# A feed-forward block's first chunk: two block products and the first out-projection matmuls are tied to a later place in TensorE's order

## The chip, the cores and the metric

The kernel runs on one core of one Trainium2 chip. The metric is the device time of one execution in microseconds (us), lower is better. Five things work side by side on the core: TensorE (PE in the profile, with PEld for its weight loads), VectorE (DVE), ScalarE (ACT), GpSimd (POOL) and SyncE (SP, which issues most loads). Each takes its own instructions in the order in which they stand, and waits at an instruction until what it needs is done.

## What is computed

One inference step of a two-layer encoder for 640 frames: 512 of a new stream and 8 times 16 of running streams. Layer 0 is a convolution module, layer 1 attends to shared keys and values, and each is followed by a SwiGLU feed-forward block. The change touches the feed-forward block alone:

```
def swiglu_ffn(h, g, w_in, w_out):
    a, b = jnp.split(rms_norm(h, g) @ w_in, 2, axis=-1)
    return h + (jax.nn.silu(a) * b) @ w_out
```

With D_MODEL = 1024 and FFN_HIDDEN = 2816, in float32. The block runs twice (once a layer).

## The kernel before

**Precision.** Every float32 product is three matmuls on parts that TensorE takes at full speed: a matrix is split into a high part (ACT copies it to a rounded type, line 374) and a low part (DVE subtracts, line 375), and hi*hi, lo*hi and hi*lo are summed in PSUM (line 442). The high and low parts of inputs are called XH and XL, of weights whi/wlo or shi/slo, of hidden tiles hid.

**Tiling.** `ffn` works on 22 hidden tiles of 128 features. Tiles 0 to 17 stand in three chunks of six, and each chunk is followed by its part of the out-projection. The two halves of the frames (320 columns each) and the two halves of the model dimension form a 2 by 2 block product, which is done with seven block products in place of eight (Strassen and Winograd's scheme, on combined inputs X11, X21, XT1 to XT4, X22). A block product is 4 k-steps of 3 matmuls: 12 matmuls of 128x320.

**Tiles 0 to 2** of the first chunk are done the plain way (`std`), since the combined inputs are not yet there. **Tiles 3, 4 and 5** are the first that use `seven`. One call of `seven` writes its block products in this order, with those of the tile ahead woven in: X11; XT4 of the tile ahead; X21; X22 of the tile ahead; XT2; XT1; XT3. The sums stand in two PSUM tiles: `pa` takes X11, then XT2 on top of it, then XT3, then XT4; `pe` takes XT1, then X22. Between them ACT copies `pa` out (`keep`, line 454): t1 after X11, t2 after XT2, t3 after XT3. Thus XT3 must not start before ACT has read t2, and XT4 not before it has read t3.

**Weights.** Each of these tiles brings 1 MB of weights (`raw`, one of two buffers, loaded by SP at line 417). DVE combines them in place (lines 425, 426, 428) with a sum `s` that POOL's two loads form (lines 420, 421), and ACT and DVE split the seven results into 11 small slots, used in turn. A raw buffer is loaded anew when its last reader is through. The third of these loads (tile 5) goes into the buffer of tile 3, then come the loads of the out-projection, of 768 KB each: group 0 into tile 4's buffer, group 1 into tile 5's, group 2 into group 0's, and so on.

**Order.** The code does not set each engine's order by itself. A scheduler orders each engine's instructions by priority and by a model of when each is ready; `tc.high_priority` lifts some, and `with behind(ins)` or `tc.issue_after(ins)` puts those of the block behind `ins` on the same engine, without a wait. The out-projection's own order is the table QORD, each step tied behind the one before by `last`; its first step in the table, `50'`, has none ahead.

Of the kernel before, what the change touches and what calls it, by code (L numbers as in the profile page):

```python
# [60 lines left out]
X11, X21, XT2, XT1, XT3, XT4, X22 = range(7)  # L61
# [24 lines left out]
def tile_trunk(ctx, tc, xT, vecs, hist, w_pw1, w_pw2, w_in0, w_out0, w_os0, w_in1, w_out1, w_os1,  # L86
# [21 lines left out]
    def mmt(n=512):  # L108
        return mm.tile([P, n], F32, tag="mm", name=nm("mm"))
# [29 lines left out]
    @contextmanager  # L139
    def behind(*ins):  # L140
        with ExitStack() as st:
            for i in ins:
                st.enter_context(tc.issue_after(i))
            yield
# [191 lines left out]
    def ffn(l, w_in, w_out, w_os, tail, hf, lead=(), b0=None, last_sum=()):  # L336
# [76 lines left out]
        def w_seven(src, out=False, first=(), rest=()):  # L413
            n = src.shape[-1] // 4
            raw, ws = wraw(), {}
            s1 = wx.tile([P, 512], F32, tag="s1", name=nm("s1"))[:, :n]
            nc.sync.dma_start(raw[:, :4 * n], src)
            a12, a11, a21, a22 = (raw[:, n * i:n * i + n] for i in range(4))
            with tc.high_priority(offset=HP), behind(*ties()):
                nc.gpsimd.dma_start(s1, src[:, 2 * n:3 * n])  # L420
                nc.gpsimd.dma_start(s1, src[:, 3 * n:4 * n], accum_op=add)
                for x in ((XT1, X11, X21, XT2, X22, XT3, XT4) if out else
                          (X11, X21, XT2, XT1, XT3, XT4, X22)):
                    if x == XT2:
                        nc.vector.tensor_tensor(out=a21, in0=a11, in1=a21, op=add)  # L425
                        nc.vector.tensor_tensor(out=a11, in0=s1, in1=a11, op=add)
                    elif x == X22:
                        nc.vector.tensor_tensor(out=a12, in0=a12, in1=a11, op=add)  # L428
                    ws[x] = slot()
                    with behind(*(first if x == XT1 else rest)):  # L430
                        cut(*ws[x], {XT1: s1, X11: a11, X21: a12, XT2: a11, X22: a12, XT3: a21,
                                     XT4: a22}[x])
            return ws

        def product(pt, w, xs, first, ks=None):
            (hi, lo), o0 = w
            n = len(xs)
            for k in ks or range(n):
                xh, xl = xs[k]
                c = slice(o0 + k * P, o0 + k * P + P)  # L440
                for i, (wt, v) in enumerate(((hi[:, c], xh), (lo[:, c], xh), (hi[:, c], xl))):
                    last = nc.tensor.matmul(pt, wt, v, start=(first and k == i == 0),  # L442
                                            stop=(k == n - 1 and i == 2), skip_group_check=True)
            return last

        def xproduct(pt, w, x, first):
            return product(pt, w, [(XH[x][:, k, :], XL[x][:, k, :]) for k in range(4)], first)
# [3 lines left out]
        def keep(tag, pt):  # L451
            t = tp.tile([P, NH], F32, tag=tag, name=nm(tag))
            with tc.high_priority(offset=HP):
                keeps.append(nc.scalar.activation(out=t, in_=pt, func=AF.Copy).ins)  # L454
            return t

        def plus(t, pt):
            with tc.high_priority(offset=HP):
                nc.vector.tensor_tensor(out=t, in0=pt, in1=t, op=add)  # L459

        def silu(t, src):
            with tc.high_priority(offset=HP):
                nc.scalar.activation(out=t, in_=src, func=AF.Silu)
# [27 lines left out]
        def combined(HH, HL, kp, second, held, neg, early=None):  # L491
# [32 lines left out]
                        own(XT4, b21)  # L524
            return sink

        def seven(src, sink, before):
            ws = w_seven(src)
            pa, pb = mmt()[:, :NH], mmt()[:, :NH]
            xproduct(pa, ws[X11], X11, True)  # L530
            t1 = keep("t1", pa)
            before(0)
            xproduct(pb, ws[X21], X21, True)
            plus(t1, pb)
            silu(t1, t1)
            before(1)
            xproduct(pa, ws[XT2], XT2, False)
            t2 = keep("t2", pa)
            pe = mmt()[:, :NH]
            xproduct(pe, ws[XT1], XT1, True)  # L540
            xproduct(pa, ws[XT3], XT3, False)
            t3 = keep("t3", pa)
            plus(t3, pe)

            def after(i):
                if i == 0:
                    last = xproduct(pa, ws[XT4], XT4, False)
                    sink(0, t1, pa)
                else:
                    last = xproduct(pe, ws[X22], X22, False)  # L550
                    plus(t2, pe)
                    silu(t2, t2)
                    sink(1, t2, t3)
                return last

            return after

        def out_chunk(c, HH, HL, after):
            ws, pts = {}, {}
            prod = {5: ("e", XT1, True, 1, 1), 1: ("a", X11, True, 0, 0),  # L560
                    2: ("b", X21, True, 0, 0), 6: ("a", XT2, False, 1, 0),
                    3: ("e", X22, False, 1, 0), 7: ("a", XT3, False, 1, 1),
                    4: ("a", XT4, False, 0, 1)}

            def go(i, u, part):
                if u not in ws:
                    o = (4 * c + u) * 12 * P
                    ws[u] = w_seven(w_os[:, o:o + 12 * P], True,
                                    (keeps[2:3], keeps[-2:-1])[u] if c == 0 and u < 2 else (),
                                    keeps[-1:] if (c, u) == (0, 1) else ())  # L570
                b, x, first, half, row = prod[i]
                if first and part != '"':
                    pts[b, u] = mmt()[:, :NH]
                pt = pts[b, u]
                with tc.issue_after(last[0]) if last else nullcontext():
                    ins = product(pt, ws[u][x], list(zip(HH[x], HL[x])), first,
                                  {"": None, "'": (0, 1), '"': (2,)}[part])
                last[:] = [ins.ins]
                if part == "'":
                    return  # L580
                hv = h[:, 2 * u + row, half * NH:half * NH + NH]
                with tc.high_priority(offset=HP):
                    nc.vector.tensor_tensor(out=hv, in0=hv, in1=pt, op=sub if row else add)  # L583

            last = []
            for t in QORD.split():
                if t[0] == "a":
                    with tc.issue_after(last[0]):
                        last[:] = [after(int(t[1])).ins]
                else:  # L590
                    go(int(t[0]), int(t[1]), t[2:])
            return lambda i: go((7, 4)[i], 3, "")
# [79 lines left out]
        for c in range(NCH):  # L672
            for jj in range(NSTD if c == 0 else 0, CW):
                if jj % 2 == 0:
                    held = [None] * 3
                if jj == NSTD and c == 0:
                    held = helds[1]
                after = seven(w_in[CW * c + jj], combined(HH, HL, jj // 2, jj % 2, held, True),
                              after)
            after = out_chunk(c, HH, HL, after)  # L680
            HH, HL = {}, {}
        hids = [(two(2 * jj), two(2 * jj + 1)) for jj in range(FT - NCH * CW)]
        for jj, hid in enumerate(hids):
            after = seven(w_in[NCH * CW + jj], plain(hid), after)
# [420 lines left out]
    for _ in ffn(0, w_in0, w_out0, w_os0, GR, hf, last_sum=last_sum)[1]:  # L1105
        pass
# [527 lines left out]
    for i in range(SPREAD_AT, KT):  # L1634
        with tc.issue_after(end):
# [4 lines left out]

    hf = ExitStack()
    spare, products = ffn(1, w_in1, w_out1, w_os1, ((256, 384), (0, 256)), hf,
                                     [(split_end[0], i) for i in (adds[1], adds[3], adds[5], sq_end)] +
                                     [(eps_end,)] * 2,
# [73 lines left out]
    last = [next(products) for _ in range(KT)][-1:]  # L1718
# [116 lines left out]
```

## Time and profile before

| | |
|---|---|
| median of 3 runs | 1445.59 us (1443.12 to 1446.67) |
| profiled execution | 1445.22 us, span 1443.4 us, granted TensorE clock 0.998 |
| PE busy | 1420.6 us (98%) |
| DVE busy | 1118.9 us (78%) |
| ACT busy | 748.6 us (52%) |
| first chunk, tiles 3 to 5 | from 285 us (first block), from 1051 us (second block) |

The first line of a page counts busy time. For a matmul that is a modelled time from start to end (0.31 us here), while the next one starts 0.147 us later, so a busy share near 100% says that PE is seldom idle for long and not that each matmul costs 0.31 us. Lost time on PE is therefore read from the distance of two starts. In a timeline a number in brackets is the engine's idle time ahead of that instruction, with what ended it; in a chain of waits each piece is what the end waited for at that time.

### The profile page before, as it was taken

How to read it: one execution, taken by the hardware profiler on the slowest of the kernel's cores; microseconds unless marked ns; L12 is line 12 of the kernel's file. 1: busy time of each engine (PE TensorE's matmuls, PEld its weight loads, DVE VectorE, ACT ScalarE, POOL GpSimd, SP SyncE). 2: the span in 40 equal slices, each digit the busy share in tenths (PEclk: the TensorE clock that was granted, in tenths of full speed). 3: DMA queues.
4: the chain of work that ended last, by engine and by line, in shares of the span. 5: the costliest groups of instructions: out<-in, count | busy, mean ns of one | idle time of the engine just before them, and what ended most of it. 6: DMA issues, size and time to landing. Idle time of an engine off the chain costs nothing. (4 is left out here: it accounts for less than half of the span.)

```text
span 1443.4 us, 28243 instructions
## 1 busy us (share of the span) xinstructions
PE 1420.6 (98%) x11086; PEld 1366.8 (95%) x11086; DVE 1118.9 (78%) x2490; ACT 748.6 (52%) x1633; POOL 284.3 (20%) x335
## 2 busy tenths in 40 slices
PE   9999999999999999999999999999999999999998
PEld 8998799999999999999998898988999999999998
DVE  6789867899788788766666756667899788888755
ACT  5666554564554554445654454543654564554443
POOL 5689221011111111013111111110011111111101
PEclk9999999999999999999999999999999999999999
DMA  7267524054435444524555555562034544444522
GB/s 246 70 174 190 137 76 135 24 141 134 138 103 143 133 110 122 146 91 162 174 183 195 191 176 166 183 220 67 30 98 134 157 111 123 132 116 124 148 60 74
DMA packets 66934, 192.58 MB, mean 133 GB/s; under 512 B 12145, under 2 KB 30321, under 8 KB 58481
## 3 DMA queue, kind: packets, MB, share of 16 engines
q1 hardware_dynamic: 52432, 160.58, 34.2%
q0 software_dynamic: 13504, 29.37, 10.3%
q8 instruction: 87, 1.43, 0.4%
q10 hardware_dynamic: 864, 0.83, 0.2%
q14 instruction: 47, 0.38, 0.1%
HBM read 179.14 MB, written 11.61 MB: 132 GB/s over the span
## 5 line engine op out<-in xcount | busy, mean ns | idle before, releaser
L442 PE MATMUL mm<-XH,whi 128*128 128x320 f32 x896 | 275.9, 310 | 2.6 <-ACT t L454 2.6
L442 PE MATMUL mm<-XH,wlo 128*128 128x320 f32 x896 | 276.3, 309 | 0.0
L442 PE MATMUL mm<-XL,whi 128*128 128x320 f32 x896 | 274.6, 309 | 0.0
L374 ACT ACTIVATE whi<-raw 128x512 fp32r<-128x512 f32 (+2 forms) x280 | 168.7, 613 | 139.4 <-PE mm L442 109.6
L375 DVE TENSOR_TENSOR wlo<-raw,whi 128x512 fp32r<-128x512 f32 (+2 forms) x280 | 184.6, 667 | 22.3 <-ACT whi L374 21.0
L442 PE MATMUL mm<-hid,whi 128*128 128x320 f32 x732 | 172.0, 310 | 3.7 <-DVE hid L375 2.7
L442 PEld LDWEIGHTS mm<-XH,whi 128*128 128x128 f32 x896 | 167.8, 188 | 4.2 <-ACT t L454 4.2
L442 PEld LDWEIGHTS mm<-XH,wlo 128*128 128x128 f32 x896 | 168.2, 188 | 0.0
L442 PEld LDWEIGHTS mm<-XL,whi 128*128 128x128 f32 x896 | 167.7, 188 | 0.0
L442 PEld LDWEIGHTS mm<-hid,whi 128*128 128x128 f32 x732 | 124.9, 188 | 6.4 <-DVE hid L375 3.7
L202 PE MATMUL mm<-xh,whi 128*128 128x320 f32 (+2 forms) x416 | 129.3, 313 | 1.0 <-ACT xh L190 0.6
L203 PE MATMUL mm<-xh,wlo 128*128 128x320 f32 (+2 forms) x416 | 128.0, 310 | 0.0
L204 PE MATMUL mm<-xl,whi 128*128 128x320 f32 (+2 forms) x416 | 126.0, 310 | 0.0
L442 PE MATMUL mm<-hid,wlo 128*128 128x320 f32 x366 | 113.0, 309 | 0.0
L442 PE MATMUL mm<-XH,shi 128*128 128x320 f32 x344 | 106.0, 309 | 0.7 <-DVE h L1548 0.7
L442 PE MATMUL mm<-XH,slo 128*128 128x320 f32 x344 | 106.0, 308 | 0.0
L442 PE MATMUL mm<-XL,shi 128*128 128x320 f32 x344 | 105.5, 308 | 0.0
L420 POOL DMA_DIRECT2D s<-in_w_in x38 | 22.1, 582 | 375.8 <-DVE wlo L375 152.8
L844 POOL TENSOR_TENSOR ca<-ca,cvt 128x512 f32<-128x512 f32 x60 | 91.8, 1531 | 17.4 <-ACT cvt L841 10.9
L374 ACT ACTIVATE shi<-raw 128x512 fp32r<-128x512 f32 (+1 forms) x114 | 66.7, 588 | 45.1 <-PE mm L442 39.6
L454 ACT ACTIVATE t<-mm 128x320 f32<-128x320 f32 x114 | 49.5, 434 | 66.8 <-PE mm L442 66.5
L583 DVE TENSOR_TENSOR h<-h,mm 128x320 f32<-128x320 f32 x168 | 79.9, 481 | 5.3 <-PE mm L442 5.1
(337 smaller groups left out, 3696.7 us busy)
## 6 DMA issues: line engine op xcount, KB each, us to landing
raw<-in_w_in SPq DMA_DIRECT2D x38, 1024.0 KB
s<-in_w_in POOLq DMA_DIRECT2D x76, 256.0 KB, 4.2
raw<-in_w_os SPq DMA_DIRECT2D x24, 768.0 KB
cache<-in_ck SPq DMA_DIRECT2D x32, 512.0 KB
cache<-in_cv SPq DMA_DIRECT2D x32, 512.0 KB
raw<-in_w_pw SPq DMA_DIRECT2D x11, 1024.0 KB
s<-in_w_os POOLq DMA_DIRECT2D x48, 192.0 KB, 3.6
raw<-in_w_kq SPq DMA_DIRECT2D x8, 1024.0 KB
```

The source lines that it names most:

```text
L202: nc.tensor.matmul(ps, wh, xh, start=(first and i == 0), stop=False)
L203: nc.tensor.matmul(ps, wl, xh, start=False, stop=False)
L204: end = nc.tensor.matmul(ps, wh, xl, start=False, stop=(stop and i == last))
L374: put_end[1] = nc.scalar.activation(out=hi, in_=src, func=AF.Copy).ins
L375: put_end[0] = nc.vector.tensor_tensor(out=lo, in0=src, in1=hi.bitcast(F32), op=sub).ins
L420: nc.gpsimd.dma_start(s1, src[:, 2 * n:3 * n])
L442: last = nc.tensor.matmul(pt, wt, v, start=(first and k == i == 0), stop=(k == n - 1 and i == 2), skip_group_check=True)
L454: keeps.append(nc.scalar.activation(out=t, in_=pt, func=AF.Copy).ins)
L583: nc.vector.tensor_tensor(out=hv, in0=hv, in1=pt, op=sub if row else add)
L844: nc.gpsimd.tensor_tensor(out=acc, in0=acc, in1=pr, op=ALU.add)
```

## The change

Three ties are added, and each has effect in the first chunk of both blocks. No instruction is added or removed.

```
--- before.py
+++ after.py
@@ -524,6 +524,12 @@
+        xt2_end, xt3_end = [], [None]
+
+        def tie(own):
+            xt2_end.append(own)
+            return {2: xt2_end[:1], 3: xt2_end[2:]}.get(len(xt2_end), ())
+
         def seven(src, sink, before):
...
@@ -534,11 +540,12 @@
             before(1)
-            xproduct(pa, ws[XT2], XT2, False)
+            own = xproduct(pa, ws[XT2], XT2, False).ins
             t2 = keep("t2", pa)
             pe = mmt()[:, :NH]
-            xproduct(pe, ws[XT1], XT1, True)
-            xproduct(pa, ws[XT3], XT3, False)
+            with behind(*tie(own)):
+                xproduct(pe, ws[XT1], XT1, True)
+            xt3_end[0] = xproduct(pa, ws[XT3], XT3, False).ins
             t3 = keep("t3", pa)
             plus(t3, pe)
@@ -582,7 +589,7 @@
-            last = []
+            last = [xt3_end[0]]
             for t in QORD.split():
```

Tile 4's XT1 now stands behind tile 3's XT2; tile 5's XT1 behind its own XT2; the out-projection's first step behind XT3 of the chunk's last tile. In later chunks the order comes out as before.

On PE, at XT3 of tile 3 in the second block: `mm_12638` is `pa` of tile 3, `mm_12819` is `pe` of tile 4, XH_1414 is XT2, XH_1416 is XT3, XH_1412 is XT1. Before:

```order
L442 MATMUL mm_12638<-XH_1414_12038,shi_12073 128x320
L442 MATMUL mm_12638<-XH_1414_12038,slo_12074 128x320
L442 MATMUL mm_12638<-XL_1415_12039,shi_12073 128x320
L442 MATMUL mm_12638<-XH_1416_12040,whi_12065 128x320 [waits Activation_49]
L442 MATMUL mm_12638<-XH_1416_12040,wlo_12066 128x320
```

The same place now:

```order
L442 MATMUL mm_12819<-XH_1412_12036,whi_12067 128x320
L442 MATMUL mm_12819<-XH_1412_12036,wlo_12068 128x320
L442 MATMUL mm_12819<-XL_1413_12037,whi_12067 128x320
L442 MATMUL mm_12638<-XH_1416_12040,whi_12065 128x320 [waits Activation_49]
L442 MATMUL mm_12638<-XH_1416_12040,wlo_12066 128x320
```

XT2 of tile 3 moved ahead of the 12 matmuls of tile 4's XT1, which now stand between XT2 and XT3 of tile 3. In the same way, 6 out-projection matmuls now stand between XT3 and XT4 of tile 5, where XT4 followed XT3 at once. Further, 8 matmuls of tile 5's X11 and X21 moved ahead of tile 4's XT3.

DVE's order follows, since the scheduler plans with PE's. On DVE in the second block, `raw_12847` is the raw buffer of tile 5, `raw_12980` that of the out-projection's group 0. The stretch up to the last reader of `raw_12847`, before:

```order
L428 TENSOR_TENSOR raw_12847<-raw_12847 128x512 [waits DVE_49]
L375 TENSOR_TENSOR slo_12070<-raw_12980,shi_12069 128x384 [waits Activation_49]
L375 TENSOR_TENSOR wlo_12066<-raw_12847,whi_12065 128x512 [waits Activation_49]
L459 TENSOR_TENSOR t_1514_12844<-mm_12819,t_1514_12844 128x320 [waits Activation_49]
L482 SCALAR_TENSOR_TENSOR B_1511_12792<-t_1502_12680,t_1504_12707 128x320 [waits Activation_49]
L426 TENSOR_TENSOR raw_12980<-s_1530_12981,raw_12980 128x384 [waits DVE_49]
L459 TENSOR_TENSOR t_1519_12883<-mm_12870,t_1519_12883 128x320 [waits PE_49,Activation_49]
L375 TENSOR_TENSOR wlo_12068<-raw_12847,whi_12067 128x512 [waits Activation_49]
```

and now:

```order
L428 TENSOR_TENSOR raw_12847<-raw_12847 128x512 [waits DVE_49]
L459 TENSOR_TENSOR t_1502_12680<-mm_12682,t_1502_12680 128x320 [waits PE_49]
L375 TENSOR_TENSOR wlo_12066<-raw_12847,whi_12065 128x512 [waits Activation_49]
L375 TENSOR_TENSOR wlo_12066<-s_1516_12848,whi_12065 128x512 [waits Activation_49]
L375 TENSOR_TENSOR hid_12244<-B_1510_12760,hid_12243 128x320 [waits Activation_49]
L375 TENSOR_TENSOR wlo_12068<-raw_12847,whi_12067 128x512 [waits Activation_49]
```

The last reader now stands ahead of five others (slo, t_1514, B_1511, raw_12980, t_1519). Its buffer takes group 1's weights (`raw_13100`) next.

Further on, DVE takes up group 2's weights (`raw_13203`), with the first two additions into h behind. Before:

```order
L428 TENSOR_TENSOR raw_13100<-raw_13100 128x384 [waits DVE_49]
L375 TENSOR_TENSOR wlo_12068<-raw_13100,whi_12067 128x384 [waits Activation_49]
L425 TENSOR_TENSOR raw_13203<-raw_13203 128x384 [waits DMAHW3_49]
L583 TENSOR_TENSOR h<-h,mm_13002 128x320 [waits PE_49]
L583 TENSOR_TENSOR h<-h,mm_13062 128x320 [waits PE_49]
```

and now (line 583 is 590 in the changed file):

```order
L428 TENSOR_TENSOR raw_13100<-raw_13100 128x384 [waits DVE_49]
L425 TENSOR_TENSOR raw_13203<-raw_13203 128x384 [waits DMAHW3_49]
L375 TENSOR_TENSOR wlo_12068<-raw_13100,whi_12067 128x384 [waits Activation_49]
L590 TENSOR_TENSOR h<-h,mm_13002 128x320 [waits PE_49]
L590 TENSOR_TENSOR h<-h,mm_13062 128x320 [waits PE_49]
```

The low part `wlo_12068` moved behind the instruction that waits for the load, ahead of the two additions. The take-up of group 1 (`raw_13100`, line 425) moved ahead too, by six places. SP's and POOL's orders are the same as before. The first block shows the same pieces with other numbers.

## The prediction

> **What bounds the kernel now.** The page first: PE is nearly always occupied, so only its gaps and what ends them can give time.
>
> ```profile
> PE 1420.6 (98%) x11086; PEld 1366.8 (95%) x11086; DVE 1118.9 (78%) x2490; ACT 748.6 (52%) x1633; POOL 284.3 (20%) x335
> ```
>
> Then PE's waits in the second block's first chunk (1058 to 1101 us): what, total us, times, longest. They add up to 2.7 us, and only the first row is for the copies that the change speaks of; the others wait for DVE's results.
>
> ```profile
> PE mm L442 <- ACT t L454: 1.1, 2, 0.5
> PE mm L442 <- DVE h L583: 0.8, 1, 0.8
> PE mm L442 <- DVE hid L375: 0.5, 1, 0.5
> PE mm L442 <- ACT hid L374: 0.3, 1, 0.3
> ```
>
> PE's timeline shows the first kind: XT2's last matmul and XT3's first two (first block), and XT4's first (second block).
>
> ```profile
> 297.15 0.31 PE L442 MATMUL mm<-XL,shi 128*128 128x320 f32 x1
> 297.98 0.41 PE L442 MATMUL mm<-XH,whi 128*128 128x320 f32 x1 [0.53 <-ACT t L454]
> 298.23 0.31 PE L442 MATMUL mm<-XH,wlo 128*128 128x320 f32 x1
> 298.38 0.31 PE L442 MATMUL mm<-XL,whi 128*128 128x320 f32 x1
> ...
> 1086.88 0.42 PE L442 MATMUL mm<-XH,whi 128*128 128x320 f32 x1 [0.53 <-ACT t L454]
> ```
>
> Undisturbed, starts are 0.147 us apart (298.23 to 298.38 reads 0.15). Here the distances are 0.83 and 0.25: a gap costs 0.69 + 0.10 = 0.79 us. There are four (XT3 of tile 3 and XT4 of tile 5, in two blocks): 3.2 us if PE alone decided.
>
> It doesn't. The chain of waits, second block:
>
> ```profile
> 1061.24 7.85 DMA raw<-in_w_in
> ...
> 1077.22 0.40 DVE B L482
> 1077.62 0.47 DVE raw L426
> 1078.09 0.40 DVE t L459
> 1078.49 0.61 DVE wlo L375
> ...
> 1079.12 5.47 DMA raw<-in_w_os
> ...
> 1087.41 5.70 DMA raw<-in_w_os
> ...
> 1098.75 103.56 PE mm L442 x703
> ```
>
> From 1061 to 1098.75 the end hangs on DVE and on loads that DVE's last readers release, PE in it only afterwards. The rows give DVE's pace too: 0.40 us for 320 columns, 0.47 for 384, 0.60 for 512.
>
> **The change, part by part.** It adds and removes no instruction; all cost is in waits.
>
> *XT2 of tile 3 goes ahead of 12 matmuls.* XT2 ends 12 x 0.147 = 1.76 us earlier, with two effects. First, ACT's copy of t2 is done before XT3 is due, behind the 12 matmuls: 0.79 us of PE gap goes in each block. The cover lasts 1.76 us, and the copy takes 0.44 (row 297.49). Second, ACT stands at that copy, with a weight split queued behind it for which DVE waits:
>
> ```profile
> 297.49 0.44 ACT L454 ACTIVATE t<-mm 128x320 f32<-128x320 f32 x1 [4.85 <-PE mm L442]
> 297.82 0.62 ACT L374 ACTIVATE shi<-raw 128x512 fp32r<-128x512 f32 x1
> ```
>
> In DVE's timeline of the second block that is the idle time at 1064.58; it goes 1.76 us earlier:
>
> ```profile
> 1064.58 0.69 DVE L375 TENSOR_TENSOR slo<-raw,shi 128x512 fp32r<-128x512 f32 x1 [2.17 <-ACT shi L374]
> ...
> 1069.11 0.69 DVE L425 TENSOR_TENSOR raw<-raw 128x512 f32<-128x512 f32 x1 [0.97 <-DMA raw<-in_w_in]
> 1069.78 0.69 DVE L375 TENSOR_TENSOR wlo<-raw,whi 128x512 fp32r<-128x512 f32 x1
> ...
> 1086.83 0.55 DVE L375 TENSOR_TENSOR wlo<-raw,whi 128x384 fp32r<-128x384 f32 x1
> ...
> 1093.13 0.56 DVE L425 TENSOR_TENSOR raw<-raw 128x384 f32<-128x384 f32 x1 [0.61 <-DMA raw<-in_w_os]
> 1093.61 0.88 DVE L583 TENSOR_TENSOR h<-h,mm 128x320 f32<-128x320 f32 x2
> ```
>
> But at 1069.11 DVE waits for tile 5's load, issued at 1061.24, when nothing has moved yet. So in the second block the 1.76 us only lengthen that wait. Gain on DVE there: nothing.
>
> *Second block from 1069.78.* DVE is dense to the end of this stretch, so its order alone counts. Up to the last reader of tile 5's raw buffer stand now 13 instructions, 9 x 0.60 + 3 x 0.40 + 0.47 = 7.07 us: it ends at 1076.9 (before, 1078.49 + 0.61 = 1079.1). Group 1's load is issued 2.2 us earlier and lands at 1076.9 + 5.5 = 1082.4 to 1082.5. But its take-up (line 425) also stands six places earlier: 12 instructions on, 8 x 0.40 + 4 x 0.47 = 5.08 us, at 1082.0. DVE waits some 0.5 us there, with all its work queued behind. Then come ten instructions and the take-up itself (4.8 us) up to the last reader of group 0's buffer: it ends at 1087.4, where it ended before (1086.83 + 0.55). That must be so: the same work from 1069.78, less one instruction of 0.40, plus the wait. Group 2's load is thus issued as before, and lands as before at 1093.1. Ahead of the additions into h now stands one `wlo` more (0.47), which before was done while DVE idled for 0.61. The additions come 0.45 us later, and PE, which waits for h and hid there, goes on 0.45 us later. With loads of 5.9 us (below, 312.31 to 318.21) it would be 1.0 later; with loads that land before DVE comes, 1.1 us earlier (the 0.40, the 0.61 and some 0.1 more). I take 0.45, since both loads have their own rows in this block.
>
> *6 matmuls between XT3 and XT4 of tile 5* cover 0.88 us, more than the 0.79. In the second block ACT's copy of t3 may be late:
>
> ```profile
> 1084.43 0.53 ACT L374 ACTIVATE whi<-s 128x384 fp32r<-128x384 f32 x1 [0.48 <-DMA s<-in_w_os]
> ...
> 1086.38 0.44 ACT L454 ACTIVATE t<-mm 128x320 f32<-128x320 f32 x1 [0.65 <-PE mm L442]
> ```
>
> Ahead of it ACT waits for POOL's load of s, and two more instructions follow, each behind DVE; so XT4 starts near 1086.5, not at 1085.4. PE's gain up to here (0.4 instead of 1.6 us) is anyway lost at the additions. The same holds of the 8 matmuls of tile 5 that go ahead of tile 4's XT3: they bring its copy and XT4 close (some 0.5 us of new wait in the second block), at no price while DVE decides.
>
> *First block.* Same chain, other state: DVE's rows, and SP's two issues.
>
> ```profile
> 301.96 0.69 DVE L425 TENSOR_TENSOR raw<-raw 128x512 f32<-128x512 f32 x1
> 302.79 0.69 DVE L375 TENSOR_TENSOR wlo<-raw,whi 128x512 fp32r<-128x512 f32 x1
> ...
> 318.21 0.56 DVE L425 TENSOR_TENSOR raw<-raw 128x384 f32<-128x384 f32 x1 [0.46 <-DMA raw<-in_w_os]
> ...
> 320.43 0.55 DVE L375 TENSOR_TENSOR wlo<-raw,whi 128x384 fp32r<-128x384 f32 x1
> ...
> 322.83 0.49 DVE L482 SCALAR_TENSOR_TENSOR B<-t,mm 128x320 f32<-128x320 f32 x1 [0.58 <-PE mm L442]
> ...
> 326.31 0.55 DVE L425 TENSOR_TENSOR raw<-raw 128x384 f32<-128x384 f32 x1
> 326.78 0.88 DVE L583 TENSOR_TENSOR h<-h,mm 128x320 f32<-128x320 f32 x2
> ```
>
> ```profile
> 312.31 0.33 SPq L417 DMA_DIRECT2D raw<-in_w_os  x1
> ...
> 321.02 0.33 SPq L417 DMA_DIRECT2D raw<-in_w_os  x1
> ```
>
> At 301.96 DVE didn't wait, so the load had landed; when, no row tells. DVE will come at 300.2. The gain is between 0 (landed just then) and 1.76. In the second block the same load needed all of 7.85 us, so I take it near the late end: 302.4 in place of 302.79 for the next row, 0.4 us. From there the work is 320.98 - 302.79 = 18.2 us, less the wait of 0.46, small ones of 0.1 and one instruction (0.40): 17.25. With a new wait of 0.45 at group 1's load (309.5 + 5.5 against DVE at 314.55), group 0's buffer is free at 320.1, 0.9 us earlier. Group 2's load needs at most 326.31 - 321.02 = 5.3 us. DVE comes at 324.8 (the wait of 0.58 for PE goes, since XT4 ends earlier), finds the load at 324.8 to 325.4, and begins the additions at 325.95 with the extra `wlo`, against 326.78: 0.8 us earlier. The ends: 1.6 (PE's two gaps, no more) and 0.1.
>
> *Sum.* -0.8 + 0.45 = -0.4 us, between -2.7 (-1.6 - 1.1) and +0.9 (-0.1 + 1.0). In later chunks PE runs without such waits (103.56 us in the last row of the chain), so what it has at the first chunk's end it keeps. Against the profiled execution's own 1445.2 us: 1444.8. The median of the runs is 0.4 higher, within their scatter of 1443.1 to 1446.7, which is added to the range.
>
> **The rivals.**
>
> *PE decides.* If the loads are there whenever DVE comes, all four gaps go and DVE's results come in time: -3.2, 1442.0. For it: the gaps are plain in the rows and PE's order is fixed when the kernel is built. Against: 0.97 us of waiting at 1069.11.
>
> *The out-projection's loads land sooner.* Issued 2.2 us earlier, group 1's load runs with less beside it. From 5.0 us down, neither load holds DVE up long: -1.6 and -1.1, together -2.7, 1442.5. Against: 5.47, 5.70 and 5.90 us in rows with different neighbours. The Trainium skill (DMA: Bandwidth & Descriptors, section on the anatomy of one DMA) gives, measured for loads of POOL's kind, about 2.0 us plus the bytes at 436 GB/s; taken for SP's loads that is an estimate of 3.8 us for 768 KB. By that rule this rival would hold in both blocks; the trace's rows are 1.7 us and more above it, so it gets little.
>
> *Slower: the early neighbour.* With the split at 1064.58 goes the last reader of tile 4's buffer, so group 0's load is also issued 1.76 us earlier, into tile 5's load, on which DVE waits. If the two share evenly for 1.76 us more, tile 5's weights land up to 0.88 later in each block: second block +1.3, first +0.1, together +1.4, 1446.6. It decides as soon as DVE's take-up comes later than 1069.5. The Trainium skill's same page (section on queues and rings) says that each DMA engine consumes one queue's descriptors in ring order. Both loads come from SP, so by that rule the early neighbour takes nothing; no row here settles it.
>
> **How the numbers follow.** Forecast 0.5; PE decides 0.15; sooner loads 0.12; early neighbour 0.18; something else 0.05. 1444.8 is the forecast's. The range reaches from the two gains to the neighbour, each with half the runs' scatter cut off: 1441.8 to 1447.2; the forecast's own is 1442.5 to 1446.1. A change of 0.3% (4.3 us) is about what a measurement of this kernel can tell. No case reaches it; the first two come within 1.6 us of it, with scatter: faster 0.06, slower 0.04, within 0.9.
>
> **What would show it.** Right: in both blocks no gap ahead of tile 3's XT3; DVE's split at 1064.58 about 1.8 us earlier, and its wait for tile 5's load in the second block near 2.7 us; a DVE wait of some 0.5 at group 1's take-up, and of 1 us at group 2's; PE's waits for h and hid in the second block longer by 1 to 2 us. Wrong: tile 5's load taken up clearly before or after 1069.1 (on the old time scale), or loads of 768 KB under 5 us, or PE waiting at places not named.

## The result and the profile after

| | before | changed |
|---|---|---|
| median of the timed runs | 1445.48 us | 1443.11 us |
| profiled execution's span | 1443.4 us | 1441.9 us |
| ratio | | 0.9985, 95% interval 0.998 to 0.9991 |

By the ratio the change gains 2.2 us, between 1.3 and 2.9 us (the two medians differ by 2.4). The forecast was a gain of 0.4, the lower bound of its sum a gain of 2.7: the sign was right, the size was not.

The page's first line and one of its groups, of the changed kernel. The last two columns of a group are the idle time of the engine just before these instructions, and what ended most of it:

```profile
PE 1420.6 (99%) x11086; PEld 1368.0 (95%) x11086; DVE 1119.8 (78%) x2490; ACT 749.3 (52%) x1633; POOL 283.5 (20%) x335
...
L442 PE MATMUL mm<-XH,whi 128*128 128x320 f32 x896 | 275.0, 310 | 0.5 <-ACT t L454 0.5
```

The same group before:

```profile
L442 PE MATMUL mm<-XH,whi 128*128 128x320 f32 x896 | 275.9, 310 | 2.6 <-ACT t L454 2.6
```

PE's waits for ACT's copies fell from 2.6 to 0.5 us: the four gaps are gone. In PE's waits in the second block's first chunk (1057 to 1105 us) no copy stands any longer, but h stands twice:

```profile
PE mm L442 <- DVE h L590: 1.2, 2, 0.8
PE mm L442 <- DVE hid L375: 0.5, 1, 0.5
PE mm L442 <- ACT hid L374: 0.3, 1, 0.3
```

The second of these two doesn't stand in the profile before. It is here in PE's timeline, behind the first additions:

```profile
1102.40 0.42 PE L442 MATMUL mm<-hid,whi 128*128 128x320 f32 x1 [0.80 <-DVE h L590]
```

Its start stands 1.12 us behind the one before it, where 0.15 is usual. DVE's timeline of the same stretch shows the rows that the prediction spoke of, and what is late at 1102.40:

```profile
1062.24 0.69 DVE L375 TENSOR_TENSOR slo<-raw,shi 128x512 fp32r<-128x512 f32 x1 [0.40 <-ACT shi L374]
...
1066.80 0.56 DVE L375 TENSOR_TENSOR wlo<-s,whi 128x384 fp32r<-128x384 f32 x1 [1.06 <-ACT whi L374]
1067.68 0.69 DVE L425 TENSOR_TENSOR raw<-raw 128x512 f32<-128x512 f32 x1 [0.32 <-DMA raw<-in_w_in]
...
1074.83 0.68 DVE L375 TENSOR_TENSOR wlo<-raw,whi 128x512 fp32r<-128x512 f32 x1
...
1080.52 0.55 DVE L425 TENSOR_TENSOR raw<-raw 128x384 f32<-128x384 f32 x1
...
1090.08 0.56 DVE L425 TENSOR_TENSOR raw<-raw 128x384 f32<-128x384 f32 x1
1090.56 0.55 DVE L375 TENSOR_TENSOR wlo<-raw,whi 128x384 fp32r<-128x384 f32 x1
1091.02 0.88 DVE L590 TENSOR_TENSOR h<-h,mm 128x320 f32<-128x320 f32 x2
...
1099.66 0.56 DVE L425 TENSOR_TENSOR raw<-raw 128x384 f32<-128x384 f32 x1 [2.34 <-DMA raw<-in_w_os]
```

SP issued the loads behind these take-ups (tile 5, then groups 1, 2 and 3) at:

```profile
1060.66 0.33 SPq L417 DMA_DIRECT2D raw<-in_w_in  x1
...
1075.54 0.33 SPq L417 DMA_DIRECT2D raw<-in_w_os  x1
...
1085.44 0.33 SPq L417 DMA_DIRECT2D raw<-in_w_os  x1
...
1093.73 0.33 SPq L417 DMA_DIRECT2D raw<-in_w_os  x1
```

The last reader at 1074.83 releases group 1's load at 1075.54. DVE takes it up 4.98 us later at 1080.52 and waits for nothing. The forecast had it land after 5.5 us, with a wait of 0.5 us. Group 2's load is there when DVE comes, 4.64 us after its issue (1090.08), where before it needed 5.70. So DVE doesn't wait from 1067.68 to the additions at 1091.02. That takes 23.34 us; before it took 24.50 (1069.11 to 1093.61). The next load takes 5.93 us, and DVE stands at its take-up for 2.34 us with additions queued behind.

The first block, the same rows of DVE:

```profile
301.67 0.69 DVE L425 TENSOR_TENSOR raw<-raw 128x512 f32<-128x512 f32 x1 [1.57 <-DMA raw<-in_w_in]
...
314.51 0.55 DVE L425 TENSOR_TENSOR raw<-raw 128x384 f32<-128x384 f32 x1
...
324.47 0.56 DVE L425 TENSOR_TENSOR raw<-raw 128x384 f32<-128x384 f32 x1 [0.38 <-DMA raw<-in_w_os]
325.41 0.88 DVE L590 TENSOR_TENSOR h<-h,mm 128x320 f32<-128x320 f32 x2
```

Here the same way takes 23.74 us, before 24.82 (301.96 to 326.78): 1.1 us less again.

**Where the time went.** PE does the same number of matmuls in nearly the same order in both kernels. So the start of each can be set against that of the same number in the trace before; the difference, followed through the trace, shows at which place PE wins or loses. It stands at -0.6 us where the first block's chunk begins (scatter between two executions). Then come -0.8 and -0.8 at the two gaps, +0.8 at the additions and +0.3 at group 3's take-up: -0.48 over the chunk. In the second block: -0.8 and -0.8, -0.4 at the additions, +1.1 at the new stall: -0.93. Between the blocks 1.0 us is lost at one place, where only the clock differs (last section). Below, "PE's balance" of a chunk is this difference from its start to its end.

### The profile page after: what moved, and what is told of

Read it like the earlier page. It is cut to its first block, busy times and chain, and to the rows that moved or that the text cites. A ratio compares the mean times of both kernels' runs of the same rounds, so it can differ in the third digit from the quotient of the medians.

```text
span 1441.9 us, 28247 instructions
## 1 busy us (share of the span) xinstructions
PE 1420.6 (99%) x11086; PEld 1368.0 (95%) x11086; DVE 1119.8 (78%) x2490; ACT 749.3 (52%) x1633; POOL 283.5 (20%) x335
## 4 chain that ended last, share of the span: by engine, by line
PE 84%; DVE 9%; DMA 4%; ACT 1%; issue 1%; POOL 1%; DVEq 0%; POOLq 0%; ACTq 0%
PE mm L442 42%; PE mm L1279 10%; PE mm L202 6%; PE mm L204 6%; PE mm L203 6%; PE mm L895 3%; DMA raw<-in_w_os 2%; PE w L1279 2%; DVE wlo L375 2%; DMA raw<-in_w_in 2%; PE am L1452 1%; PE am L1524 1%; PE am L1468 1%; PE w L1423 1%; DVE slo L375 1%
```

## Experiments

Theory A: DVE and the loads that it waits for set the end of the chunk. The gain is group 1's load, which is issued earlier and so runs clear of POOL's loads. Theory B: PE's own gaps are the gain. PE's balance, worked out from each trace against that of the kernel before, in us:

| kernel | block 1 | block 2 | timed ratio, 95% interval |
|---|---|---|---|
| the whole change | -0.48 | -0.93 | 0.9985 (0.998 to 0.9991) |
| out-projection's tie only | +0.13 | +0.82 | 0.9993 (0.9984 to 1.0002) |
| both block products only | -0.24 | -1.80 | 0.997 (0.9959 to 0.9982) |
| whole change, first block only | -1.00 | (+0.09) | 0.9986 (0.9977 to 0.9995) |
| whole change, second block only | (+0.22) | -1.44 | 0.9982 (0.9973 to 0.9991) |
| late last reader | +1.09 | -0.31 | 0.999 (0.9981 to 1.0) |
| group 3 taken up later | -1.30 | -2.08 | 0.9972 (0.9961 to 0.9983) |
| groups 2 and 3 later | -1.54 | -2.29 | 0.9971 (0.996 to 0.9981) |
| products only, group 2 later | -1.46 | -1.28 | 0.9965 (0.9953 to 0.9978) |
| light s loads | (+0.43) | (+0.15) | one run, 1444.86 us |
| group 3 later, no tie | -0.56 | -0.70 | 0.9994 (0.9985 to 1.0003) |
| tile 4's tie only | -1.36 | -1.51 | 0.9985 (0.9977 to 0.9994) |

In brackets are blocks with the order of before: they differ by up to 0.4 us by chance, and no single balance means more than that. Added up over both blocks, a kernel's balances miss its timed gain by up to 2.3 us (both block products only: -2.0 against -4.4). Averaged over the blocks that have the order of before (three each) and over those that have the order of the change (two each), the change wins 0.96 us in the first block and 1.26 in the second: 2.2 in all, the size of the timed gain.

**The out-projection's tie only.**

```
-            return {2: xt2_end[:1], 3: xt2_end[2:]}.get(len(xt2_end), ())
+            return ()
```

> Only the out-projection's first step is tied behind XT3 of tile 5; both block products stay where they were. On PE six matmuls move between XT3 and XT4 of tile 5, in both blocks, and no other engine's order changes. Theory A (DVE and the loads it waits for set the end of the first chunk, and the gain of the whole change comes from their order): the two gaps of 0.79 us ahead of XT4 go, PE waits as much longer for h right behind them, and the time stays: 0 us, within 0.3. Theory B (PE's own gaps are the gain): -1.6 us.

It gave 0.9993, -1.0 us (-2.3 to 0.3), which excludes neither. The edit was a poorer test than I thought. Its six matmuls stood ahead of XT3 of tile 5 before, and covered the copy of t2 there. In PE's timeline of the second block a new gap stands at XT3, and the wait for h at the additions swallows what is left:

```profile
1082.33 0.42 PE L442 MATMUL mm<-XH,whi 128*128 128x320 f32 x1 [0.29 <-ACT t L454]
...
1093.69 0.42 PE L442 MATMUL mm<-hid,shi 128*128 128x320 f32 x1 [1.84 <-DVE h L590]
```

DVE's order is that of before, and there is no gain in either block. That speaks for A, but group 2's load also happened to be late in this profile, which accounts for most of the 1.84:

```profile
1092.28 0.56 DVE L425 TENSOR_TENSOR raw<-raw 128x384 f32<-128x384 f32 x1 [1.67 <-DMA raw<-in_w_os]
```

**Both block products only.**

```
-            last = [xt3_end[0]]
+            last = []
```

> Only the two block products are tied (XT1 of tiles 4 and 5); the out-projection's first step is free as before. Up to the take-up of group 1's weights DVE's order is that of the whole change; PE keeps part of the gap ahead of XT4 of tile 5 (two matmuls of cover, 0.3 of 0.79 us). Theory A: about the whole change, -1.5 to -2.2 us, and group 1's load lands within 5.0 us of its issue. Theory B: the two gaps ahead of XT3 of tile 3 and 0.3 us of each other one: -2.2 us less what is given back. The trace decides: by A what PE has at its first wait for h is what DVE brings; by B it is the sum of its gaps.

It gave 0.997, a gain of 4.4 us (2.6 to 5.9), twice that of the whole change and more than either theory had forecast. Group 1's load was taken up 4.97 us after its issue in both blocks, as A had it. DVE's order is the same up to group 1's take-up; the scheduler put group 3's take-up three places later, behind two more additions. The experiments with the take-ups follow that up.

**One block at a time.**

```
-            return {2: xt2_end[:1], 3: xt2_end[2:]}.get(len(xt2_end), ())
+            return {2: xt2_end[:1], 3: xt2_end[2:]}.get(len(xt2_end), ()) if l == 0 else ()
...
-            last = [xt3_end[0]]
+            last = [xt3_end[0]] if l == 0 else []
```

and the same with `l == 1`.

> The whole change in the first block alone, the second as before. The prediction's sum: -0.8 us. From the two traces, aligned matmul by matmul: -0.9 us at the first block's end, nothing more behind. If the first block's gain were lost on the way to the second (the profile of the changed kernel gives back 1.0 us between 1000 and 1005 us): 0.

> The whole change in the second block alone, the first as before. The prediction's sum: +0.45 us. If loads that land sooner are what it missed: -0.9 us (PE 1.6 earlier at XT4 of tile 5, 2.0 at the first additions, 1.0 given back at the next group's load), with group 1's load of 768 KB taken up within 5.0 us of its issue.

Both gain: -2.0 us (-3.3 to -0.7) and -2.6 us (-3.9 to -1.3). The forecast of +0.45 for the second block alone is excluded. The two add up to more than the whole change did (-4.6 against -2.2); their traces add up to -2.4. What of this is scatter stays open. In the first block of the first kernel, which has the changed order, the 0.8 us that the changed kernel's profile loses at the additions is not lost: PE's start there is 0.24 us late, as before, in place of 1.04.

The first of these kernels has the old order in its second block. Its DVE rows there, for the take-ups of tile 5 and of groups 1, 2 and 3:

```profile
1067.31 0.69 DVE L425 TENSOR_TENSOR raw<-raw 128x512 f32<-128x512 f32 x1
...
1082.86 0.55 DVE L425 TENSOR_TENSOR raw<-raw 128x384 f32<-128x384 f32 x1
...
1091.52 0.55 DVE L425 TENSOR_TENSOR raw<-raw 128x384 f32<-128x384 f32 x1
...
1100.33 0.56 DVE L425 TENSOR_TENSOR raw<-raw 128x384 f32<-128x384 f32 x1 [2.05 <-DMA raw<-in_w_os]
```

In the profile before, the first and the third of these showed waits of 0.97 and 0.61 us. Here neither has one, and the fourth waits 2.05 in place of 0.84. The fourth in the profile before, second block and first:

```profile
1100.74 0.56 DVE L425 TENSOR_TENSOR raw<-raw 128x384 f32<-128x384 f32 x1 [0.84 <-DMA raw<-in_w_os]
...
334.89 0.56 DVE L425 TENSOR_TENSOR raw<-raw 128x384 f32<-128x384 f32 x1 [1.81 <-DMA raw<-in_w_os]
```

The instructions are the same, and so is the end of the chunk within 0.1 us. Waits for loads of this kind pass from one take-up to another between executions of the same order. The second block's 0.84 was the exception: in six of the eight blocks that keep DVE's order of before, DVE waits 1.8 to 2.2 us at group 3's take-up, and PE's start behind it is 0.4 to 0.9 us late. In the four blocks with the order of the change PE is 0.7 to 1.0 us late there. So the stall at group 3 is new against this one profile, not against the order of before.

**The late last reader.** The split of tile 5's X22 weights is written behind the sum of its t1:

```
+                    if held is not None and x == X22:
+                        held.append((ws[x], a12))
+                        continue
...
-            plus(t1, pb)
+            p = plus(t1, pb)
+            if held:
+                with tc.high_priority(offset=HP), behind(p):
+                    cut(*held[0][0], held[0][1])
```

> The whole change, but the split of X22's weights of tile 5 (the last reader of its raw buffer) is written behind the sum of tile 5's t1, so that on DVE it stands some seven places later, about where it stood before the change; DVE's take-up of group 1 stands where it stood before, and POOL issues group 2's first load of s ahead of group 1's second. PE's order of block products is that of the whole change, all four gaps gone. Theory A (the gain is group 1's load, issued 2.2 us earlier and so clear of POOL's own loads: packets for 2.6 us in place of 3.8 to 4.2): the load is issued some 2.5 us later, runs beside POOL's loads again and is taken up 5.0 us or more after its issue; the additions come as late as before, and of -2.2 us at most -0.8 is left. Theory B (PE's gaps): as the whole change, -2.2 us.

Group 1's load was issued at 311.50 and taken up 6.21 us later, with a wait:

```profile
317.71 0.56 DVE L425 TENSOR_TENSOR raw<-raw 128x384 f32<-128x384 f32 x1 [0.73 <-DMA raw<-in_w_os]
```

In the second block it took 5.64 us (1077.15 to 1082.79). That is as A says. In time it gave 0.999 (0.9981 to 1.0), -1.4 us. That interval, -2.7 to 0, holds the forecasts of both theories; the balances lose 1.6 and 0.6 us against it. In the first block this kernel has a loss of its own, a wait of 1.98 us for the copy of t3, so the size isn't group 1's load alone.

**Light s loads**, to test the reason for the load's duration by itself, in the kernel before:

```
-                nc.gpsimd.dma_start(s1, src[:, 3 * n:4 * n], accum_op=add)
+                nc.gpsimd.dma_start(s1[:, :m], src[:, 3 * n:4 * n][:, :m], accum_op=add)
```

with `m` = 16 for the out-projection's groups 1 and 2 of the first chunk.

> The kernel before, but POOL's accumulating load of s in the out-projection's groups 1 and 2 of the first chunk brings 16 of 384 columns in place of all (s is then wrong in the rest: it is for the loads' times alone). No engine's order changes. Theory A (group 1's load is slow because POOL's loads of s run beside it): in both blocks its packets take 2.6 to 3.3 us, as in the changed kernels, in place of 3.8 and 4.2, and it is there when DVE comes (no wait of 0.46 in the first block). If the duration hangs on something else, as the hour or the engines' work: 3.8 to 4.9 us as in the kernel before and in the one with the late reader. The time itself should move by less than 1 us.

The DMA view of the stretch in which group 1's load ran, first the kernel before (second block, 1080.2 to 1084.2 us); columns are packets, MB and share of the 16 engines, q1 is SP's queue and q0 POOL's:

```profile
DMA packets 312, 1.11 MB, mean 277 GB/s; under 512 B 32, under 2 KB 154, under 8 KB 312
...
q1 hardware_dynamic: 144, 0.79, 62.5%
q0 software_dynamic: 168, 0.32, 36.5%
```

With the light s loads (1079.0 to 1082.0 us):

```profile
q1 hardware_dynamic: 144, 0.79, 83.0%
q0 software_dynamic: 170, 0.15, 19.7%
```

With the whole change (1076.7 to 1079.5 us):

```profile
q1 hardware_dynamic: 144, 0.79, 77.7%
q0 software_dynamic: 37, 0.08, 7.5%
```

And with the late last reader (first block, 312.4 to 317.4 us):

```profile
q1 hardware_dynamic: 144, 0.79, 59.4%
q0 software_dynamic: 267, 0.37, 43.3%
```

The same 144 packets of 0.79 MB take 3.8 us beside 0.32 MB of POOL's, 2.9 beside 0.15, 2.6 beside 0.08 and 4.9 beside 0.37. The second of these has every engine's order of the first; only POOL's accumulating loads are lighter. Over all traces, by first and last packet of group 1's load (the last column counts every packet of POOL's that overlaps it; the views count those that begin in their window, and so show less):

| where the load stands | blocks | packets' time | issue to last packet | POOL's data beside it |
|---|---|---|---|---|
| early last reader | 14 | 2.6 to 3.3 us | 3.8 to 4.5 us | 103 to 163 KB |
| old place, or late reader | 10 | 3.8 to 4.9 us | 4.8 to 5.9 us | 181 to 375 KB |
| old place, light s loads | 2 | 2.9 and 3.3 us | 3.95 and 4.26 us | 126 and 182 KB |

The ranges of the first two don't meet (3.3 against 3.8 us, and 4.5 against 4.8). That POOL's loads of s make group 1's load slow is shown. Their bytes alone don't give the size: beside 181 KB one load of the second row took 3.9 us, beside 182 KB one of the third took 3.3.

**Group 3's take-up later**, a version for the stall that gave half of the gain back:

```
+                        with behind(*take):
+                            nc.vector.tensor_tensor(out=a21, in0=a11, in1=a21, op=add)
...
+                                    adds[4:5] if (c, u) == (0, 3) else ())
```

where `adds` lists the additions into h.

> The whole change, and DVE's take-up of group 3's weights in the first chunk tied behind the fifth addition into h: it moves four places, behind one split and two additions. If the new stall of PE (gaps of 0.9 and 1.1 us behind the wait of 2.1 to 2.3 us for that load, one in each block) is where the change gives its gain back: 0.75 + 0.96 us of it go, so -2.2 - 1.7 = -3.9 us against the kernel before, as the two block products alone measured (-4.4), where the scheduler put the take-up at this very place. If the load's lateness only moves the wait a few places on: -2.2, as the whole change.

It gave 0.9972: -4.0 us (-5.6 to -2.5), as expected. DVE's rows (line 590 is 592 here):

```profile
1093.40 0.88 DVE L592 TENSOR_TENSOR h<-h,mm 128x320 f32<-128x320 f32 x2
1094.81 0.56 DVE L426 TENSOR_TENSOR raw<-raw 128x384 f32<-128x384 f32 x1 [0.53 <-DMA raw<-in_w_os]
```

Two additions now go ahead of the wait, and PE's second wait for h in this chunk is gone (1053 to 1101 us):

```profile
PE mm L443 <- DVE hid L375: 0.5, 1, 0.5
PE mm L443 <- DVE h L592: 0.3, 1, 0.3
PE mm L443 <- ACT hid L374: 0.3, 1, 0.3
```

**Groups 2 and 3 later**: the tie `adds[1:2]` for group 2 as well.

> As the take-up of group 3 tied later, and group 2's take-up (DVE waits there for its load, 0.4 us in the first block) tied behind the first two additions as well, for which PE waits 0.4 to 1.2 us in both blocks. If DVE's order there holds the additions up: the two stalls of PE for h become 0.4 to 0.9 us shorter each, and half of it is lost again at the hidden tiles behind (PE's next waits, 0.6 and 0.8 us, are for those): 0.5 us better than with group 3's take-up alone, -4.4 us. If the hidden tiles decide: the same -3.9 us.

It gave 0.9971, -4.2 us (-5.8 to -2.7), no more than group 3 alone; the interval holds both forecasts. In the first block's trace PE's wait for h went down to a distance of 0.34 us between two starts, and the next one, for ACT's part of the hidden tile, grew to 1.04. That speaks for the hidden tiles as what decides there.

**Products only, group 2 later**: the same two take-ups without the out-projection's tie.

> The two block products tied and the out-projection free, with group 2's take-up behind the first two additions; group 3's stands behind the fifth by the scheduler's own choice. Six matmuls between XT3 and XT4 of tile 5 or two: if PE's gap there counts, 0.5 us a block slower than the same take-ups with the out-projection tied; if DVE decides, the same: -4.4 us by both of the other terms, -3.4 by the first.

It gave 0.9965 (0.9953 to 0.9978). The out-projection's tie is worth nothing measurable here, though the interval, -6.8 to -3.2 us, still holds the -3.4. This and the three kernels with group 3's take-up late and both products tied lie at -4 to -5 us and can't be told from each other. By their medians all four beat both kernels of the case; the interval of this one alone doesn't meet that of the whole change.

**Group 3's take-up later, no tie.**

> The kernel before, with DVE's take-up of group 3's weights tied behind the fifth addition, and none of the three ties. If the take-up stands in the way whether the block products are tied or not, it gives here what it gave there (-1.7 us). If it is the ties that bring PE to the additions so early that the wait for group 3's load shows: only the first block's stall of 0.43 us (gap 0.579 less 0.147) goes, the second block's profile has none, and the time falls by 0.4 us.

It gave 0.9994 (0.9985 to 1.0003), -0.9 us, with a balance of -0.56 and -0.70. The interval, -2.2 to 0.4 us, excludes neither forecast. By the balances the take-up stood in the way before, too, for about a third of what the ties and the take-up gain together (-1.3 of -3.4). The expectation of no gain in the second block had taken the profile before for the rule, where group 3's load made DVE wait for 0.84 us only.

**Tile 4's tie only.**

```
-            return {2: xt2_end[:1], 3: xt2_end[2:]}.get(len(xt2_end), ())
+            return {2: xt2_end[:1]}.get(len(xt2_end), ())
...
-            last = [xt3_end[0]]
+            last = []
```

> Only XT1 of tile 4 is tied (behind XT2 of tile 3); tile 5's XT1 and the out-projection are free. DVE's last reader of tile 5's raw stands early, and its take-up of group 3 late, as with both products tied; on PE the gap ahead of XT4 of tile 5 may stay. Theory A (DVE's order and the loads decide): as with both products tied, -3.9 to -4.4 us. Theory B (each gap of PE counts): 0.8 to 1.6 us less than that, -2.8 or so.

DVE's early last reader and late take-up of group 3 are there, and so is the gap ahead of XT4 of tile 5:

```profile
1084.70 0.41 PE L442 MATMUL mm<-XH,whi 128*128 128x320 f32 x1 [0.53 <-ACT t L454]
...
1092.05 0.41 PE L442 MATMUL mm<-hid,shi 128*128 128x320 f32 x1 [0.49 <-DVE h L590]
```

PE then waits for h as if the gap had not been, and the balance (-1.36 and -1.51) is close to that with group 3's take-up later in the first block and 0.6 short of it in the second. In the first block that is A, in the second it lies between the two. The time is nearer to B: 0.9985, -2.2 us (-3.3 to -0.9), which excludes A's -3.9 to -4.4 and holds B's -2.8. Later chunks have another order in this kernel as well; whether the rest is lost there was not tried.

## Why the prediction was right in sign and wrong in size

- **The four gaps of PE** went, all of them, as the prediction's rival "PE decides" had it. The forecast's late copy of t3 in the second block and the 0.5 us of new wait at tile 4's XT4 didn't come: no start there is later than usual.
- **The split 1.76 us earlier** was right: its wait fell from 2.17 to 0.40 us. Part of it came back as a wait of 1.06 us for ACT at 1066.80.
- **Tile 5's load unmoved in the second block** was the profile's own chance. It was taken up 7.02 us after its issue in place of 7.85, with its neighbour issued only 2.30 us behind it in place of 4.06. In the first block it was 7.11 us with the close neighbour, and 7.75 in the first block of the kernel with the light s loads, where the neighbour is as far as before. Over all traces, from issue to its last packet, it took 5.2 to 7.5 us with the far neighbour (10 blocks) and 5.4 to 7.8 with the close one (16 blocks), 6.6 on average in both. So the rival of the early neighbour found no cost. By the Trainium skill (DMA: Bandwidth & Descriptors, section on queues, rings and completion order) each DMA engine consumes one queue's descriptors in ring order. The traces agree in that the neighbour costs nothing; they don't show the rings.
- **Second block, "I take 0.45, since both loads have their own rows in this block"** is the step that failed. Its mechanism, a load of unchanged duration that DVE must wait for, did not hold. The rows, 5.47 and 5.70 us, belonged to the place in which the loads stood and to that one execution. Released 2.2 us earlier, group 1's load ran beside 0.08 MB of POOL's in place of 0.32 and was there before DVE came. With that the prediction's own lower end holds: 1.1 us was forecast for it, 1.16 measured (24.50 less 23.34).
- **First block, -0.8**: the additions came 0.78 us earlier, on a scale on which PE reaches the chunk at the same time in both traces. But that is luck, since other parts gave it than those forecast. Tile 5's load gained nothing (taken up at 301.67, 0.3 later on the same scale), and there was no wait of 0.45 at group 1's load; the 1.1 us did it here too.
- **"What it has at the first chunk's end it keeps"** ended the chunk too early. It counted to the first additions; 10 us later DVE stands at group 3's take-up, and PE, now earlier, ran into it. About 1 us of the second block's 2.0 was given back there, measured against the one profile before, whose wait at this place was short.
- **The rival "loads land sooner"** with its -2.7 came nearest. Two of the three rows held against it, 5.47 and 5.90 us, came from loads with 0.30 and 0.37 MB of POOL's beside them. The Trainium skill (DMA: Bandwidth & Descriptors, section on the anatomy of one DMA) has a rule, fitted to loads of POOL's kind, of 2.0 us plus the bytes at 436 GB/s, an estimate of 3.8 us for 768 KB. The prediction set it aside as too low by 1.7. Group 1's loads clear of POOL's took 3.8 to 4.5 us from issue to last packet, and where DVE waited for a load of 768 KB it went on 0.3 to 0.6 us after the last packet. So the rule comes nearer for these than for the others (4.8 to 5.9), and is still low.
- **The prediction's own signs of being wrong** stood in the trace: loads of 768 KB under 5 us (4.98 and 4.64), and PE waiting at a place not named (1102.40). DVE's wait for tile 5's load in the second block, named as near 2.7 us, was 0.32.

## What to carry to other kernels

Before a load's duration is carried to a new place in the program, look up in the DMA view what ran beside it in the old place and what will run beside it in the new one, and take a wait that one profile shows for a draw (0.97, 0.61 and 0.84 us in one execution, 0, 0 and 2.05 in another of the same order). Follow a gain until the queue behind it is past its next load. An instruction that waits for a load belongs behind those whose results another engine needs; here that took the gain from 2.2 to 4.0 us, with intervals that just overlap.

## What the runs showed of the hardware

- SP's loads get slower beside POOL's: 768 KB took 2.6 us of packets nearly alone (0.08 MB beside it) and 4.9 us beside 0.37 MB. The Trainium skill (DMA: Bandwidth & Descriptors, section on queues, rings and completion order) says that each DMA engine goes round-robin between the queues at packet granularity. The traces agree in that both queues move data at once, and don't show the turns. The cost is larger than the bytes alone: 0.29 MB more took 2.3 us more, where at the rate of the faster load (0.79 MB in 2.6 us) they would be 1.0 us.
- Group 3's load took 4.9 to 5.7 us from issue to last packet in twelve of the blocks with the early reader, beside 11 to 77 KB of POOL's data, and 4.3 and 3.9 us in the two blocks with tile 4's tie only, beside 2 KB and none. So little data beside it is not enough to explain a whole microsecond by its bytes; what makes it slow there is not settled.
- PE's granted clock fell to 0.50 for 3.4 us near 1000 us in six of the thirteen profiles, the one with the light s loads (the order of before) among them. The stretch from 1000 to 1005 us, in the kernel before, in the changed one and with the light s loads (the third number from the end is the granted clock):

```profile
1000.00:1005.00 5.00, 4.73 (x34) 4.41 (x33) 4.37 (x9) 0.85 (x3) 1.73 (x1) 1.00 0.79 235
```

```profile
1000.00:1005.00 5.00, 5.00 (x27) 4.64 (x26) 3.75 (x8) 1.43 (x4) 0.84 (x1) 0.75 0.99 362
```

```profile
1000.00:1005.00 5.00, 5.00 (x29) 4.80 (x28) 3.82 (x8) 1.28 (x3) 1.05 (x1) 0.79 0.95 352
```

It costs 0.7 to 1.0 us of a profiled execution, about one block's gain. So two spans of single profiles don't compare kernels at this size; the timed runs do.
